# One image of the sixth pair stored over two queues, and four small rows in place of seven

## The chip, the cores and the metric

The kernel runs on one core of a Trainium2 chip. The metric is device time of one execution in microseconds (us), the median of several executions. Lower is better.

## The reference

A dilated 3x3 convolution, written as loops:

```python
batch, c_in, h, w, c_out, k, dilation = 16, 64, 64, 64, 128, 3, 2
x_pad = np.pad(x, ((0, 0), (0, 0), (pad, pad), (pad, pad)))     # pad = 2
for b, co, ci, kh, kw in all combinations:
    output[b, co] += weight[co, ci, kh, kw] * x_pad[b, ci, kh*2:kh*2+h, kw*2:kw*2+w]
```

Input `x` is 16 images of 64 channels of 64x64 (float32, 16.8 MB), the output 16 images of 128 channels of 64x64 (float32, 33.6 MB).

## The kernel before

The 16 images are worked on as 8 pairs. A pair of inputs lies on 128 partitions (two images of 64 channels), 16 KB in each. `load(pb)` brings one pair by one DMA of 128 rows of 16 KB. ScalarE and, for some chunks, GpSimd cast it to float16 (`cast`); VectorE forms sums of row blocks (`rowsum`); for pairs 3 to 5 ScalarE and GpSimd also make shifted copies (`shift`).

Each pair is computed in 4 groups `g` of 16 rows, 32 groups `G` in all. In every group TensorE makes three products, `psP`, `psA` and `psB`. ScalarE copies `psP` to SBUF (L307). VectorE adds it to `psA` and to `psB` (L315) and writes the results into a ring `o_ring` that holds the outputs of 3 pairs: pair 7 reuses the place of pair 4, and nothing reuses the place of pair 5. The order of all this is written out by hand (`manual_schedule`).

All transfers, loads and stores, are issued by SyncE in program order. A store of one whole image (`store`, L251) has 128 rows of 16 KB, one for each output channel, which is one for each partition. `pair_store(pb)` stores the two images of a pair after the last group of the pair, image 0 and then image 1. The transfers use 8 completion semaphores in turn, so a transfer is issued only when the one issued eight places earlier on that queue has landed.

The last pair is stored in halves. Its image 1 is stored differently in the first half (32 of 64 rows of pixels): `ROWS4` pixel rows at the end of that half are cut off and stored by two DMAs of their own, one of 124 partitions and one of the last 4 (`FOUR`). With `ROWS4 = 7` the main part has rows of 6,400 bytes, and the two cut-off stores have rows of 1,792 bytes.

```python
store(pb, 1, 0, 2 * GR - ROWS4)
store(pb, 1, 2 * GR - ROWS4, 2 * GR, FOUR)
```

The last two stores, of 128 rows of 8 KB each, follow when the last group is done.

Of the kernel before, what the change touches and what calls it, by code (L numbers as in the profile page):

```python
# [10 lines left out]
def kernel(  # L11
# [7 lines left out]
    nc = tc.nc  # L19
# [9 lines left out]
    P = 128  # L29
# [5 lines left out]
    HW = H * W  # L35
    GR = 16
# [19 lines left out]
    out_img = out.rearrange("b o h w -> b o (h w)")  # L56
# [14 lines left out]
    def o_pair(pb):  # L71
        at = pb % OB * 2 * HW
        return o_ring[:, at : at + 2 * HW]
# [80 lines left out]
    def turn(k):  # L154
# [24 lines left out]
        out=x16_tiles[0][:, 8 * W : 18 * W], in_=x32_tiles[0][:, 8 * W : 18 * W]  # L179
# [41 lines left out]
    for m in range(2):  # L221
        for r in range(2):
# [3 lines left out]
                out=w_st[pp, m * KW * CO : (m + 1) * KW * CO],  # L226
                in_=w_sb[pp, kind * KW * CO : (kind + 1) * KW * CO],
# [21 lines left out]
    def store(pb, m, r0=0, r1=H, rows=((0, P),)):  # L249
        for lo, hi in rows:  # L250
            nc.sync.dma_start(  # L251
                out=out_img[2 * pb + m, lo:hi, r0 * W : r1 * W],
                in_=o_pair(pb)[lo:hi, m * HW + r0 * W : m * HW + r1 * W],
            )

    def pair_store(pb):
        for m in range(2):
            store(pb, m, GR // 4 if pb == m == 0 else 0)

    LOADS = {0: (3,), 2: (4,), 3: (5,), 7: (6,), 11: (7,)}  # L260
    FOUR = ((0, P - 4), (P - 4, P))
    ROWS4 = 7

    for G in range(ngroups):
        pb, g = divmod(G, NG)
# [48 lines left out]
        for e, ps in ((1, psB), (0, psA)) if late else ((0, psA), (1, psB)):  # L314
            nc.vector.tensor_tensor(  # L315
                out=o[:, :, b0 : b0 + NBLK, e],
# [6 lines left out]
        if g == NG - 1 and later:  # L323
            pair_store(pb)
# [4 lines left out]
        if pb == npairs - 1:  # L329
            if g % 2 == 1:  # L330
                store(pb, 0, (g - 1) * GR, (g + 1) * GR)
                if g == 1:
                    store(pb, 1, 0, 2 * GR - ROWS4)
                    store(pb, 1, 2 * GR - ROWS4, 2 * GR, FOUR)
                else:
                    store(pb, 1, (g - 1) * GR, (g + 1) * GR)
        elif g == NG - 1 and not later:
            pair_store(pb)
# [35 lines left out]
```

## Time and profile before

| what | value |
|---|---|
| median of 3 runs | 126.7 us (126.54 to 127.01) |
| the profiled execution | 126.72 us |
| its span, first to last instruction | 124.9 us |
| bytes read from HBM, written to HBM | 17.07 MB, 33.55 MB |
| PE, DVE, ACT, POOL busy | 107.7, 90.8, 69.6, 31.0 us |
| SyncE's queue of transfers, share of 16 engines' span | 96.5% |

The page of the profile gives busy time by engine, the span in 40 slices, the transfers by queue, the chain of work that ended last, and the costliest groups of instructions. Besides, the trace holds one record for each packet of the DMA engines (queue, start, duration, size; not the number of the engine) and the time of each increment that a transfer makes to its semaphore: one for each DMA engine that took part. In this trace a packet is one row of a transfer. The core has 16 DMA engines; a store of 128 rows gives 8 rows to each.

### The profile page before, as it was taken

How to read it: one execution, taken by the hardware profiler on the slowest of the kernel's cores; microseconds unless marked ns; L12 is line 12 of the kernel's file. 1: busy time of each engine (PE TensorE's matmuls, PEld its weight loads, DVE VectorE, ACT ScalarE, POOL GpSimd, SP SyncE). 2: the span in 40 equal slices, each digit the busy share in tenths (PEclk: the TensorE clock that was granted, in tenths of full speed). 3: DMA queues.
4: the chain of work that ended last, by engine and by line, in shares of the span. 5: the costliest groups of instructions: out<-in, count | busy, mean ns of one | idle time of the engine just before them, and what ended most of it. 6: DMA issues, size and time to landing. Idle time of an engine off the chain costs nothing.

```text
span 124.9 us, 2265 instructions
## 1 busy us (share of the span) xinstructions
PE 107.7 (86%) x928; PEld 53.5 (43%) x928; DVE 90.8 (73%) x103; ACT 69.6 (56%) x76; POOL 31.0 (25%) x54
## 2 busy tenths in 40 slices
PE   6889999989999999999999999999999999920000
PEld 2255555545555553444444444445555555500000
DVE  0575979759998888596969797887988988760000
ACT  4178687396666887696848496949643333300000
POOL 3483306059610003829191920000000000000000
PEclk9999999999999999999999999999999999999555
DMA  4999999999899999999999999999999999999981
GB/s 118 402 445 446 435 414 430 435 435 409 291 410 442 425 441 425 417 430 425 438 435 422 435 420 420 430 441 430 430 430 420 425 430 435 425 422 412 420 380 76
DMA packets 4322, 50.77 MB, mean 406 GB/s; under 512 B 472, under 2 KB 728, under 8 KB 1112
## 3 DMA queue, kind: packets, MB, share of 16 engines
q1 hardware_dynamic: 4312, 50.63, 96.5%
q8 instruction: 7, 0.11, 0.3%
q14 instruction: 3, 0.02, 0.0%
HBM read 17.07 MB, written 33.55 MB: 405 GB/s over the span
## 4 chain that ended last, share of the span: by engine, by line
PE 66%; DVE 1%; DVEq 1%; issue 0%
PE psB L211 25%; PE psP L211 14%; PE psA L211 14%; PE psA L237 13%; DVE osb L315 1%; DVEq L369 1%; DVEq L315 0%
## 5 line engine op out<-in xcount | busy, mean ns | idle before, releaser
L211 PEld LDWEIGHTS <-w_sb 64*128 64x128 f16 x816 | 44.7, 94 | 42.0 <-issue 4.5
L315 DVE TENSOR_TENSOR osb<-psA,p_sb 128x1024 f32<-128x1024 f32 x32 | 39.1, 1223 | 15.6 <-ACT p_sb L307 11.9
L307 ACT COPY p_sb<-psP 128x1024 f32<-128x1024 f32 x32 | 32.4, 1012 | 30.5 <-issue 16.1
L211 PE MATMUL psB<-x,w_sb 64*128 64x496 f16 (+3 forms) x384 | 45.0, 365 | 0.0
L315 DVE TENSOR_TENSOR osb<-psB,p_sb 128x1024 f32<-128x1024 f32 x32 | 39.0, 1219 | 0.4 <-ACT p_sb L307 0.3
L83 ACT CAST x<-x 128x1024 f16<-128x1024 f32 (+2 forms) x27 | 28.2, 1050 | 4.1 <-DMA x<-in_x_dram 3.9
L118 POOL COPY xo<-x 64x512 f16<-64x512 f16 (+1 forms) x36 | 22.0, 612 | 28.9 <-PE psA L237 22.0
L211 PE MATMUL psA<-x,w_sb 64*128 64x496 f16 (+2 forms) x240 | 28.2, 365 | 0.3 <-DVE x L178 0.3
L211 PE MATMUL psP<-xs,w_sb 64*128 64x496 f16 (+1 forms) x192 | 26.0, 372 | 0.6 <-ACT p_sb L307 0.5
L237 PE MATMUL psA<-xo,w_st 128*128 128x496 f16 (+1 forms) x72 | 16.3, 375 | 0.0
L95 DVE TENSOR_TENSOR xs<-x 128x512 f16<-128x512 f16 x32 | 14.4, 450 | 0.2 <-ACT x L83 0.2
L237 PEld LDWEIGHTS <-w_st 128*128 128x128 f16 x72 | 6.6, 98 | 9.3 <-issue 2.1
L116 ACT COPY xo<-x 64x512 f16<-64x512 f16 x12 | 7.4, 615 | 0.2
L85 POOL CAST x<-x 128x896 f16<-128x896 f32 (+1 forms) x4 | 3.9, 987 | 8.5 <-DMA x<-in_x_dram 8.5
L136 PE MATMUL dm<-zero 128*128 128x512 f16 x10 | 4.6, 580 | 1.2 <-DVE zero L126 1.2
L225 POOL COPY w_st<-w_sb 64x384 f16<-64x384 f16 x4 | 2.5, 632 | 1.6 <-ACT w_sb L171 1.4
L146 DVE CAST wd<-w 128x192 f16<-128x192 f32 x1 | 0.5, 501 | 2.6 <-DMA w<-in_weight_dram 2.6
L136 PEld LDWEIGHTS <-zero 128*128 128x128 f16 x10 | 1.1, 124 | 2.6 <-issue 1.3
L159 PEld LDWEIGHTS <-wd 128*64 128x64 f16 x30 | 1.1, 128 | 2.3 <-DVE wd L146 1.2
L159 PE MATMUL wt<-ident,wd 128*64 128x128 f16 x30 | 1.7, 252 | 0.3 <-DVE wd L146 0.3
L148 ACT ACT_TABLE_LOAD x1 | 1.3, 1283 | 0.7 <-PEq L355 0.7
L171 ACT CAST w_sb<-wt 128x384 f16<-128x384 f32 x1 | 0.5, 479 | 1.9 <-PE wt L159 1.9
(19 smaller groups left out, 8.0 us busy)
## 6 DMA issues: line engine op xcount, KB each, us to landing
out_dram<-osb SPq DMA_DIRECT2D x13, 2048.0 KB, 18.6
x<-in_x_dram SPq DMA_DIRECT2D x7, 2048.0 KB, 14.7
out_dram<-osb SPq DMA_DIRECT2D x3, 1024.0 KB, 12.1
out_dram<-osb SPq DMA_DIRECT2D x1, 1920.0 KB, 18.9
x<-in_x_dram SPq DMA_DIRECT2D x1, 1088.0 KB, 5.3
x<-in_x_dram SPq DMA_DIRECT2D x1, 960.0 KB, 7.1
out_dram<-osb SPq DMA_DIRECT2D x1, 800.0 KB, 13.6
w<-in_weight_dram SPq DMA_DIRECT2D x1, 288.0 KB, 2.9
```

The costliest lines, as they stand in the source:

```text
L83: eng.copy(out=out, in_=in_)
L85: eng.tensor_copy(out=out, in_=in_)
L95: nc.vector.tensor_tensor(out=s, in0=v[:, :, 0], in1=v[:, :, 1], op=add)
L116: eng.copy(out=to, in_=src)
L118: eng.tensor_copy(out=to, in_=src)
L136: nc.tensor.matmul(out=dm[:, 0:512], lhsT=zero[:, 0:P], rhs=zero)
L159: nc.tensor.matmul(out=wts[k % 3][r * CI : (r + 1) * CI, c0 + j * CO : c0 + (j + 1) * CO], lhsT=wd[:, t * CI : (t + 1) * CI], rhs=ident,)
L211: nc.tensor.matmul(out=po, lhsT=w_sb[pp, t * CO : (t + 1) * CO], rhs=rhs, start=first and j == 1, stop=last and j == 2,)
L225: nc.gpsimd.tensor_copy(out=w_st[pp, m * KW * CO : (m + 1) * KW * CO], in_=w_sb[pp, kind * KW * CO : (kind + 1) * KW * CO],)
L237: nc.tensor.matmul(out=rows(ps[:, m * NH : (m + 1) * NH])[:, :, o0:o1], lhsT=w_st[:, t * CO : (t + 1) * CO], rhs=rows(xo[:, g, m])[:, :, d ...
L307: nc.scalar.copy(out=p_sb, in_=psP)
L315: nc.vector.tensor_tensor(out=o[:, :, b0 : b0 + NBLK, e], in0=ps.rearrange("p (m b q) -> p m b q", m=2, q=2 * W), in1=pv, op=add,)
```

## The change

Image 1 of pair 5 (`SHARED`; pairs are counted from 0) is no longer stored by one DMA of 128 rows on SyncE's queue. GpSimd issues two DMAs for it, of 5 rows and of 44 rows; SyncE issues five, of 64, 4, 4, 4 and 3 rows. Every row is 16 KB as before, and every row is stored once. With the rows counted in eights, the first DMA of GpSimd takes one row from each of the first five eights, its second takes the four odd rows from each of the other eleven. SyncE's DMA of 64 takes the even rows, its three DMAs of 4 take the other three odd rows of each of the first four eights, and its DMA of 3 takes those of the fifth eight.

In the last pair `ROWS4` becomes 4: the main part of that half image has rows of 7,168 bytes instead of 6,400, and the cut-off stores have rows of 1,024 bytes instead of 1,792.

No instruction of TensorE, VectorE or ScalarE changes, nor its place. GpSimd's two DMAs stand behind its last `shift` copy; SyncE has four more DMAs, between the store of image 0 of pair 5 and those of pair 6.

```diff
+    SHARED = (5, 1)
+
+    def shared_store(pb, m):
+        dst, src = out_img[2 * pb + m], o_pair(pb)[:, m * HW : (m + 1) * HW]
+        nc.gpsimd.dma_start(out=dst[1:40:8], in_=src[1:40:8])
+        nc.gpsimd.dma_start(out=dst[41:P:2], in_=src[41:P:2])
+        nc.sync.dma_start(out=dst[0:P:2], in_=src[0:P:2])
+        for k in (3, 5, 7):
+            nc.sync.dma_start(out=dst[k:32:8], in_=src[k:32:8])
+        nc.sync.dma_start(out=dst[35:40:2], in_=src[35:40:2])
+
     def pair_store(pb):
         for m in range(2):
-            store(pb, m, GR // 4 if pb == m == 0 else 0)
+            if (pb, m) == SHARED:
+                shared_store(pb, m)
+            else:
+                store(pb, m, GR // 4 if pb == m == 0 else 0)
...
-    ROWS4 = 7
+    ROWS4 = 4
```

## The prediction

> **What bounds the kernel now.** I read the page first: the busy lines, the slices, the queues. TensorE is busy for 86% of the span, but look at the last slices.
>
> ```profile
> PE   6889999989999999999999999999999999920000
> ...
> DMA  4999999999899999999999999999999999999981
> ...
> q1 hardware_dynamic: 4312, 50.63, 96.5%
> q8 instruction: 7, 0.11, 0.3%
> q14 instruction: 3, 0.02, 0.0%
> ```
>
> TensorE stops four slices early; the DMA engines are full from the second slice to the last but one. So the transfers set the end. The stretches of time say how full:
>
> ```profile
> core 0: us, PE busy (x) PEld busy (x) DVE busy (x) ACT busy (x) POOL busy (x), PEclk, DMA share, GB/s
> ...
> 113.00:118.00 5.00, 0.00 (x0) 0.00 (x0) 0.00 (x0) 0.00 (x0) 0.00 (x0) 0.72 1.01 420
> 118.00:121.00 3.00, 0.00 (x0) 0.00 (x0) 0.00 (x0) 0.00 (x0) 0.00 (x0) 0.50 0.98 412
> 121.00:124.90 3.90, 0.00 (x0) 0.00 (x0) 0.00 (x0) 0.00 (x0) 0.00 (x0) 0.50 0.30 126
> ```
>
> The share is 1.0 until 118, and 0.30 in the last 3.9 us: the 16 engines do not end together. The waits of SyncE's queue end in the same thing; its other long waits are for results of VectorE, with a backlog of transfers in front:
>
> ```profile
> SPq L251 <- DVE xs L95: 66.5, 7, 12.9
> SPq L369 <- DMA out_dram<-osb: 10.9, 3, 6.2
> ```
>
> The chain that ended last names 66% PE. It is followed back from VectorE's last add, done at 111.4, and does not contain the landing that the end waits for, so I don't use it.
>
> **Who ends last.** The increments of the last store (one for each DMA engine) come at 120.66, 120.93, 121.24, 121.25, 121.97, 122.02, 122.42, 122.54, 122.56, 123.06, 123.28, 123.53, 123.54, 123.54, 123.82 and 124.05. The span ends 0.90 later, the time stands 1.77 over the span. To know whose these are I chained packet records: an engine's next packet starts within about 5 ns of the end of the one before, and each has eight rows of every full store. That is a reconstruction; the records carry no engine number. It gives:
> - Four engines, and only four, carry the cut-off stores (31 rows and 1 row of 1,792 bytes each; both stores made four increments). They end at 123.06, 123.53, 123.54 and 123.82.
> - Of the twelve others one is slow in its own right: from 74 to 110 its 16 KB rows take 643 ns on average, on undisturbed engines 611. It ends last, 124.05.
> - The other eleven: 123.54, 123.28, then 122.56 and earlier. Those with a late end have had an instruction fetch (the q8 line) in their way.
>
> **The change, part by part.** The engines always have work queued, so what counts is the work given to each, by the medians of the row sizes: 16 KB 611 ns, 7,680 bytes 291, 6,400 bytes 244, 1,792 bytes 74, 1,024 bytes 46.
> - Main part of the half image: 7,168 bytes come to 272 ns between 244 and 291. Eight rows x 28 ns = +0.22 us on every engine.
> - Cut-off stores: 32 rows x (46 - 74) ns = -0.90 on the first four engines.
> - The moved rows, if they fall as the diff arranges them: +0.61 on engines 0 to 2, -1.83 on engine 4 (counted by the eights of rows), none elsewhere.
> - More completion records of 9 ns each: about +0.02, on the first four +0.03.
> - GpSimd's rows: four on engines 5 to 15, one on 0 to 4, on a second queue. No row of the trace shows a store on it. Lower bound 0 extra per row: a row moves the same bytes at the 611 ns that all undisturbed rows take, so a gain is excluded beyond the few ns between packets. Upper bounds are from the only other foreign packets, the fetches: an 8 KB fetch on q14 held its engine's own packets up for 302 ns and stretched the next by 115 to 349, that is 0.11 to 0.34 more than the 0.309 of an own row of that size; a 16 KB fetch on q8 held them up for about 0.9 and stretched the next by about 0.4, 0.66 more than 0.611. I take 0.11, the smallest seen: fetches read HBM singly, these rows read SBUF as stores do and queue behind each other. Call it x; four rows make 0.44, one 0.11.
>
> Sums, x apart: engines 0 to 2 -0.03, engine 3 -0.65, engine 4 -1.59, the others +0.24.
>
> The trace doesn't say which of the twelve is the slow one; by count alone it is engine 4 in one case of twelve. So the likeliest is that it keeps its eight rows: 124.05 + 0.24 + 0.44 = 124.73, 0.68 later, 126.72 + 0.68 = **127.4**. The profiled execution stands at the median (126.7), so nothing is corrected.
>
> **A rule on the slow engine.** The row is the 643 ns above. The Trainium skill, "DMA: Bandwidth & Descriptors", section "Latency and other measured facts", says engines 7 and 15 are usually the slower ones, which speaks against this change: by it engine 4 isn't the slow one, and the sum is the 127.4 above. The trace agrees that one engine is slow and that it isn't among the first four; it can't name it.
>
> **What costs nothing, and its cover.** GpSimd is idle after 72.7, and its DMAs wait for the add of the last group of pair 5, at 87.5; nobody waits behind them. SyncE's four more issues take 0.33 to 1.12 us each, at most 5 us from 87.5, and its next wish is at 99.1. A transfer waits for the one eight places earlier on its queue, and five small ones now stand among them. Pair 6's second store waits for pair 4's second, landed at 94.81; GpSimd's rows jump the backlog and make that 2.9 later, 97.7, wanted at 99.1. The half image at 105.7 waits for the 64-row part, by 105.4. With 8 us of backlog behind, a miss of 1 us would still cost nothing. VectorE writes pair 7 over pair 4 at 99.55: 1.8 us to spare.
>
> **Rivals.**
> 1. *The slow engine doesn't count: faster.* It is the spared one (then it ends near 122.5), or it isn't slow: its rows take 611 ns again from 54 to 58, from 69 to 74 and from 110 on, so the slowness comes and goes. Then the next count: engines 0 to 2 at 123.82 - 0.03 + x, and the others at 123.54 + 0.24 + 4x. At x = 0 the end is 123.79, -0.26: 126.46, and no version of this sum gives more. At x = 0.11 it is 124.22, +0.17: 126.9. The point that decides is x = 0.07. For it: the slow engine did end last, and a place that is slow in every execution could be spared on purpose. Against: five engines stand within 0.52 of it.
> 2. *GpSimd's rows fall on other engines: slower.* The two cut-off stores, with 124 and 4 rows, used the same four engines, so SyncE's queue begins at the first each time. If GpSimd's does the same with 44 rows on eleven engines, engines 0 to 2 have 13 rows instead of 8: 123.82 - 0.64 + 3.06 + 5x = 126.2 to 126.8, the time 128.9 to 129.5. If it deals three rows to each of engines 0 to 13 and two to the next, they have 12: 123.82 - 0.64 + 2.44 + 4x = 125.6 to 126.1, the time 128.3 to 128.7. The Trainium skill, same page, "Why a DMA increments its semaphore by 16 and not by 1", gives for GpSimd's queue eleven engines going on from a cursor, which is the diff's layout, and as a measured exception rows divided by 16 and rounded up, the three to each. No run here shows which.
> 3. *A foreign row is as dear as a fetch*, x = 0.66 on engines 5 to 15: 124.05 + 0.24 + 2.64 = 126.9, the time 129.6; at 0.34 it is 128.3.
> 4. *My chaining is wrong on who is last*, and the spared engine leads by over 0.6: near 125.9.
>
> **How the numbers follow.** Half a per cent, 0.63 us, is about what a measurement of this kernel can tell from no change: the limits are 126.07 and 127.33. The forecast has 0.34; at x under 0.1 it gives 126.96 to 127.3, within the limits, which is nearly half of it. Rival 1 has 0.26, nearly all within. Rival 2 0.20, rival 3 0.12, both slower. Rival 4 0.08, faster. That makes 0.08 faster, 0.38 within (0.15 + 0.23), 0.54 slower (0.19 + 0.03 + 0.20 + 0.12). The range takes in rival 1 from 126.4 and rival 2 to 128.8, and leaves out rival 4 and the dearest of 2 and 3.
>
> **What would show it.** After the change a second data queue with 49 packets of 16 KB. Right: 7,168-byte packets at 272 ns; the last increments again spread over about 3 us, the last from an engine with rows of 643 ns; one engine some 1.9 us earlier against the rest. Rival 1: the slow engine is that one. Rival 2: three engines end 1.7 us or more after all others. Rival 3: 16 KB packets well over 611 from 88 to 100 us, or holes between them. The forecast is wrong if the time is under 126.9, or if the DMA share falls under 1.0 between 100 and 118, which would mean a wait among the issues.

## The result and the profile after

The changed kernel takes 130.82 us against 126.75 before: the ratio is 1.0305, with an interval of 1.0267 to 1.0343. That is 4.1 us slower; the forecast was 127.4, and the range ended at 128.8. The profiled execution took 130.14, its span is 128.4 (before 126.72 and 124.9), so it shows 3.4 us of the loss. Executions fall into a faster and a slower state, so every ratio in this document compares the faster ones alone, while times are medians of all; e1 below has one fast execution and so no ratio, the ratio of e6 rests on two, and the profiles of these two runs, taken in the slower state, are not read.

The page after the change, the same lines as before (slices of 3.21 us; then queue, packets, MB, share of 16 engines' span):

```profile
PE   6889999989999999999999999999999999300000
...
DMA  4999999999899999999999999999999999999830
...
q1 hardware_dynamic: 4278, 49.83, 93.2%
q0 software_dynamic: 96, 0.80, 1.6%
q8 instruction: 7, 0.11, 0.3%
q14 instruction: 3, 0.02, 0.0%
```

TensorE is busy for 107.3 us (107.7 before). There is a second data queue, q0, with 0.80 MB, which is 49 rows of 16 KB. The loss is at the end, where the engines now run out one after the other. The stretches of time after the change (columns as in the prediction; the last two are DMA share and GB/s):

```profile
113.00:118.00 5.00, 0.00 (x0) 0.00 (x0) 0.00 (x0) 0.00 (x0) 0.00 (x0) 0.51 1.00 423
118.00:121.00 3.00, 0.00 (x0) 0.00 (x0) 0.00 (x0) 0.00 (x0) 0.00 (x0) 0.50 0.98 332
121.00:124.90 3.90, 0.00 (x0) 0.00 (x0) 0.00 (x0) 0.00 (x0) 0.00 (x0) 0.50 0.48 201
124.90:128.40 3.50, 0.00 (x0) 0.00 (x0) 0.00 (x0) 0.00 (x0) 0.00 (x0) 0.50 0.06 26
```

Two things are to be seen. Until 124.9 the engines have moved less than before, and from there on almost nobody works: a share of 0.06 is one engine of sixteen on average. And from 118 to 121 the engines count as full (0.98) but move 332 GB/s instead of 412: their packets take longer. Between 118 and 121, 28 of them (mostly 8 KB ones, up to 753 ns against 309) took over 100 ns more than is usual for their size; before, none did.

The issues came when the prediction said (start, us, engine, line). First GpSimd's queue of instructions, then SyncE's:

```profile
88.01 0.67 POOL L261 DMA_DIRECT2D out_dram<-osb  x1 [15.05 <-DVE osb L330]
88.68 0.53 POOL L262 DMA_DIRECT2D out_dram<-osb  x1
```

```profile
88.12 0.58 SPq L263 DMA_DIRECT2D out_dram<-osb  x1
88.75 3.08 SPq L265 DMA_DIRECT2D out_dram<-osb  x3
91.87 0.87 SPq L266 DMA_DIRECT2D out_dram<-osb  x1
99.29 14.03 SPq L251 DMA_DIRECT2D out_dram<-osb  x8
```

SyncE's waits after the change (total, times, longest):

```profile
SPq L384 <- DMA out_dram<-osb: 13.8, 1, 13.8
...
SPq L251 <- DMA out_dram<-osb: 1.0, 1, 1.0
```

One issue waited 1.0 us for a semaphore, the miss that the prediction allowed for; the DMA share stays at 0.98 or above until 118, so it cost nothing. The 13.8 is the wait for the last landing.

**Who ends last.** The last store's increments come at 120.87, 121.34, 121.44, 121.91, 122.26, 122.40, 122.74, 122.83, 122.95, 123.77, 124.32, 124.40, and then 125.16, 125.84, 126.65 and 127.15. Chained as in the prediction, the packets say that the last four are the four engines with the cut-off stores. They also say how GpSimd's rows fell: four to each of five engines, three to each of nine, two to one and none to one. That is one row to each of the first five, and of the 44 three to each engine from the first on, until they were used up. So engines 0 to 2 store 12 rows of this image, engine 3 has 11, engine 4 eight, the next nine 7, then one 6 and one 4. Of the five with four rows four are those of the cut-off stores; the fifth is the slow engine, whose 16 KB rows average about 647 ns here. If the DMAs of 4 and of 5 rows use the engines in order from the first, as this overlap suggests, it is engine 4, the one that was to be spared, and it stores eight rows as before. The records carry no engine number, so the 4 is a count and not a reading.

### The profile page after: what moved, and what is told of

Read it like the earlier page. It is cut to its first block, busy times and chain, and to the rows that moved or that the text cites. A ratio compares the mean times of both kernels' runs of the same rounds, so it can differ in the third digit from the quotient of the medians.

```text
span 128.4 us, 2272 instructions
## 1 busy us (share of the span) xinstructions
PE 107.3 (84%) x928; PEld 53.3 (42%) x928; DVE 90.8 (71%) x103; ACT 69.6 (54%) x76; POOL 32.1 (25%) x56
## 4 chain that ended last, share of the span: by engine, by line
PE 64%; DVE 1%; DVEq 1%; issue 0%
PE psB L211 24%; PE psP L211 14%; PE psA L211 13%; PE psA L237 12%; DVE osb L330 1%; DVEq L384 1%; DVEq L330 0%
## 5 line engine op out<-in xcount | busy, mean ns | idle before, releaser
L136 PE MATMUL dm<-zero 128*128 128x512 f16 x10 | 4.1, 533 | 1.2 <-DVE zero L126 1.2
L261 POOL DMA_DIRECT2D out_dram<-osb x1 | 0.7, 673 | 15.0 <-DVE osb L330 15.0
```

Of the source, the lines that this page charges most:

```text
L136: nc.tensor.matmul(out=dm[:, 0:512], lhsT=zero[:, 0:P], rhs=zero)
```

## The experiments

| run | time, us | ratio | interval |
|---|---|---|---|
| the change | 130.82 | 1.0305 | 1.0267 to 1.0343 |
| e1_two_small_pool | 131.89 to 135.43 | - | - |
| e2_even_queues | 126.91 | 0.9997 | 0.9960 to 1.0034 |
| e3_same_load_sync | 129.72 | 1.0198 | 1.0105 to 1.0291 |
| e4_rows4_only | 126.90 | 1.0000 | 0.9966 to 1.0034 |
| e5_halves | 131.07 | 1.0284 | 1.0209 to 1.0358 |
| e6_halves_sbuf_only | 132.07 | 1.0274 | 1.0160 to 1.0389 |
| e7_halves_hbm_only | 126.69 | 0.9977 | 0.9928 to 1.0026 |
| e8_skew_at_home | 125.71 | 0.9904 | 0.9856 to 0.9952 |
| e9_as_meant | 131.77 | 1.0394 | 1.0367 to 1.0420 |
| e10_away_alone | 128.36 | 1.0115 | 1.0089 to 1.0142 |
| e11_more_skew_at_home | 126.47 | 0.9990 | 0.9959 to 1.0020 |
| e12_load_at_home | 128.25 | 1.0116 | 1.0086 to 1.0145 |

The kernel before took 126.64 to 127.05 beside them (medians). The edits below are shortened: `dst` is the image in HBM, `src` its place in SBUF. Runs e1, e2, e4 to e7 and e10 edit the kernel before, the others the changed kernel.

### The second queue by itself: e2_even_queues

```diff
-nc.sync.dma_start(out=dst, in_=src)
+nc.gpsimd.dma_start(out=dst[1:P:2], in_=src[1:P:2])
+nc.sync.dma_start(out=dst[0:P:2], in_=src[0:P:2])
```

> Edit to the kernel before: image 1 of pair 5 is stored by one DMA of 64 rows on GpSimd's queue and one of 64 rows on SyncE's, so that each DMA engine has 4 rows on each queue and 8 in all, as before. ROWS4 stays 7. Theory 1 (the loss of the change is the load of the first engines, the second queue costs nothing by itself): 126.7, within 0.3. Theory 2 (what the loss has beyond the extra rows, some 1.5 us, is the price of rows on a second queue): 127.5 to 128.5, with 16 KB packets over 611 ns or holes between packets while both queues have rows.

No change. Its page has 64 rows on the second queue, and its stretch from 92 to 100 us, when both queues have rows, runs at the full rate (the first line is the kernel before, the second e2):

```profile
q0 software_dynamic: 80, 1.05, 2.0%
```

```profile
92.00:100.00 8.00, 8.00 (x82) 4.51 (x80) 7.01 (x9) 3.04 (x3) 0.00 (x0) 1.00 1.00 424
```

```profile
92.00:100.00 8.00, 8.00 (x81) 4.36 (x78) 7.17 (x8) 2.52 (x4) 0.00 (x0) 1.00 1.00 426
```

Of the 64 rows on the second queue 59 took 611 or 612 ns and one over 650 (985, close behind an instruction fetch). So a foreign row costs nothing measurable; theory 2 falls.

### The cut-off rows by themselves: e4_rows4_only

```diff
-    ROWS4 = 7
+    ROWS4 = 4
```

> Edit to the kernel before: ROWS4 = 4 alone. By the sums of the prediction engines 0 to 3 end 0.67 earlier, all others 0.22 later; the slow engine sets the end: 124.27, the time 126.9. If instead the smaller rows of 1,024 bytes bring the stretched packets that the changed kernel shows from 118 to 121, some 1 us: 127.7.

126.90, and the profiled execution's last increment at 124.40, where 124.27 was expected. By the chained packets the slow engine ends last. That agrees with the sum, but 0.2 us is less than the time can tell from nothing (1.0000, 0.9966 to 1.0034). What the run rules out is the other expectation, 127.7: the smaller rows by themselves do not bring the stretched packets, of which the profile has two.

### The same load without GpSimd: e3_same_load_sync

```diff
-nc.gpsimd.dma_start(out=dst[1:40:8], in_=src[1:40:8])
-nc.gpsimd.dma_start(out=dst[41:P:2], in_=src[41:P:2])
+nc.sync.dma_start(out=dst[39:P:2], in_=src[39:P:2])
+nc.sync.dma_start(out=dst[1:32:8], in_=src[1:32:8])
...
-nc.sync.dma_start(out=dst[35:40:2], in_=src[35:40:2])
+nc.sync.dma_start(out=dst[33:38:2], in_=src[33:38:2])
```

> Edit to the changed kernel: GpSimd stores nothing; all rows of image 1 of pair 5 are issued by SyncE, in DMAs of 64, 45, 4, 4, 4, 4 and 3 rows, which give the engines nearly the loads seen after the change: 12 rows to engines 0 to 2, 11 to engine 3, 7 to 4 to 14, 4 to engine 15. ROWS4 is 4. Theory 1 (load of the first engines alone): as slow as the changed kernel, 130 to 130.8. Theory 2 (part of the loss is the second queue): only the extra rows remain, +1.8 on the last of the first four engines, 128.4.

129.72: about two thirds of the loss comes back with no row on GpSimd's queue (2.0%, interval 1.05 to 2.9%). But it lies between the numbers of the two theories, and its 16 KB rows are stretched too, up to 1,754 ns between 100 and 106 us. What stretches them is the question of the runs below.

### Where GpSimd's rows begin: e1_two_small_pool and e9_as_meant

```diff
-nc.sync.dma_start(out=dst, in_=src)
+nc.gpsimd.dma_start(out=dst[0:5], in_=src[0:5])
+nc.gpsimd.dma_start(out=dst[5:16], in_=src[5:16])
+nc.sync.dma_start(out=dst[16:P], in_=src[16:P])
```

> Edit to the kernel before: image 1 of pair 5 is stored by two DMAs of GpSimd, of 5 and of 11 rows, and one of SyncE of 112 rows (7 to each DMA engine). ROWS4 stays 7. Theory A, GpSimd's queue deals the rows of every DMA from the first engine: engines 0 to 4 carry 2 rows on the second queue, engines 5 to 10 one, 11 to 15 none; engines 0 to 3 have 9 rows in all, +0.61, so the last increment moves from 124.05 to about 124.5 to 124.7 and the time to 127.2 to 127.4. Theory B, small counts go on from where the DMA before ended: every engine has exactly one row on the second queue, nothing is moved, the time is 126.7 plus at most 0.1.

131.9 and more: far off both theories. It couldn't tell them apart, since its 112 rows brought in something that neither had: from 16 on, seven to an engine, they are no longer each engine's own eight. Runs e5 to e7 are about that; the question itself was put again:

```diff
-nc.gpsimd.dma_start(out=dst[1:40:8], in_=src[1:40:8])
-nc.gpsimd.dma_start(out=dst[41:P:2], in_=src[41:P:2])
+Q = HW // 4
+for k in range(4):
+    nc.gpsimd.dma_start(out=dst[1:40:8, k*Q:(k+1)*Q], in_=src[1:40:8, k*Q:(k+1)*Q])
+    nc.gpsimd.dma_start(out=dst[41+2*k:P:8], in_=src[41+2*k:P:8])
```

> Edit to the changed kernel: GpSimd's 44 rows are issued as four DMAs of 11 rows (one row of each of the eights 5 to 15), and its 5 rows in four quarters of 4 KB, one ahead of each. Theory B (a small DMA on GpSimd's queue goes on from the engine where the last one ended): engines 5 to 15 store their own rows, the slow engine 4 has 5 rows, and the load is what the change says. By the sums engines 0 to 2 end at 123.8: 126.5, faster than before by 0.2. Theory A (every DMA begins at the first engine): engines 0 to 2 have 13 rows, 126.2 and so 128.9, and with rows away from their engine 130 and more.

131.77, on theory A's side. In the chained packets the five engines with 4 KB pieces (the four of the cut-off stores and the slow one) also have four of GpSimd's 16 KB rows each: a DMA of 11 rows after one of 5 begins at the first engine again. So in none of these forms can GpSimd's queue pass over engine 4.

### Rows away from their engine: e5_halves, e6_halves_sbuf_only, e7_halves_hbm_only

```diff
+# e5: rows 0 to 63, then 64 to 127, on both sides
+nc.sync.dma_start(out=dst[0:CI], in_=src[0:CI])
+nc.sync.dma_start(out=dst[CI:P], in_=src[CI:P])
+# e6: only the partitions that are read
+nc.sync.dma_start(out=dst[0:P:2], in_=src[0:CI])
+nc.sync.dma_start(out=dst[1:P:2], in_=src[CI:P])
+# e7: only the rows that are written
+nc.sync.dma_start(out=dst[0:CI], in_=src[0:P:2])
+nc.sync.dma_start(out=dst[CI:P], in_=src[1:P:2])
```

> Edit to the kernel before: image 1 of pair 5 is stored by two DMAs of SyncE, rows 0 to 63 and rows 64 to 127. Every DMA engine has 4 + 4 rows, 8 in all as before, but not the eight rows that it has in a store of 128 rows. ROWS4 stays 7. Theory 1 (load alone): 126.7, within 0.3. Theory 3 (an engine that works on rows of another engine's eight shares a path with it, and rows stretch from 611 to 1,000 ns and more, as some of the changed kernel's do): up to 8 rows x 0.5 us on top, 128 to 131, with stretched 16 KB packets from about 102 us on.

> As the halves, but only on the side of SBUF: the sources are partitions 0 to 63 and 64 to 127, the destinations the even and the odd rows, so that each engine writes rows of its own eight in HBM (the image's channels come out in another order). Theory 1: 126.7. Theory 3 with the shared path on SBUF's side: as slow as the halves. Theory 3 with the path on HBM's side: 126.7.

> The reverse: the sources are the even and the odd partitions, each engine reading its own eight, the destinations rows 0 to 63 and 64 to 127 (the image's channels come out in another order). Theory 1: 126.7. Theory 3 with the shared path on SBUF's side: 126.7. Theory 3 with the path on HBM's side: as slow as the halves.

All three give each engine eight rows. Two are 2.7 to 2.8% slower (the one with the halves in SBUF alone by 1.6 to 3.9%), the third is not slower at all. The stretch from 100 to 106 us, before, with halves on both sides, and with halves in HBM alone:

```profile
100.00:106.00 6.00, 6.00 (x60) 3.21 (x58) 5.17 (x7) 2.02 (x2) 0.00 (x0) 1.00 1.02 431
```

```profile
100.00:106.00 6.00, 6.00 (x60) 3.25 (x58) 5.17 (x7) 2.02 (x2) 0.00 (x0) 1.00 0.98 281
```

```profile
100.00:106.00 6.00, 6.00 (x60) 3.23 (x58) 5.17 (x7) 2.02 (x2) 0.00 (x0) 1.00 1.01 426
```

All are full by their share; one moves 281 GB/s. In it 46 rows took over 711 ns, the longest 2,589. So what counts is the partitions that are read, not the rows of HBM that are written. Even and odd rows, four of each consecutive eight at a time, are at full rate (e2, e7). The reading taken here is that a row is slow when an engine reads partitions outside its own consecutive eight ("away"), because another engine reads there too. That is argued and not shown: the records don't say which engine reads which partition, and no path was measured. A rival is that a contiguous half is slow because it reads only 64 of the 128 partitions at a time. By itself it is not enough, since the 112 rows of e1 span fourteen of the sixteen eights and that run lost 5 us or more; no run here separates the two further, and the next section has rows that fit neither.

### How much of it is in the change: e10_away_alone and e12_load_at_home

```diff
+# e10: 8 rows to each engine, four of them away
+nc.gpsimd.dma_start(out=dst[33:P:2], in_=src[33:P:2])
+nc.sync.dma_start(out=dst[0:P:2], in_=src[0:P:2])
+nc.sync.dma_start(out=dst[1:32:2], in_=src[1:32:2])
+# e12: 11 rows to engines 0 to 3, 7 to the others, all read at home
+nc.sync.dma_start(out=dst[0:P:2], in_=src[0:P:2])
+nc.sync.dma_start(out=dst[1:P:4], in_=src[1:P:4])
+nc.sync.dma_start(out=dst[3:P:8], in_=src[3:P:8])
+nc.sync.dma_start(out=dst[7:32:8], in_=src[7:32:8])
+for k in range(3):
+    nc.sync.dma_start(out=dst[39+32*k:min(P,71+32*k):8], in_=src[(1,3,5)[k]:32:8])
```

> Edit to the kernel before: image 1 of pair 5 is stored by one DMA of 48 rows on GpSimd's queue (odd rows 33 to 127, three to each engine) and two of SyncE, of 64 even rows and of 16 odd rows (1 to 31, one to each). Every engine has 8 rows, but four of them of another engine's eight, as the changed kernel's three or four are. ROWS4 stays 7. Load alone: 126.7. If rows away from their engine make what the extra rows of the changed kernel leave unexplained (about 1.5 us): 127.5 to 128.5, with stretched 16 KB packets from 93 to 105 us.

> Edit to the changed kernel: image 1 of pair 5 is stored by SyncE alone, and every engine reads only partitions of its own eight: DMAs of 64, 32 and 16 rows (4, 2 and 1 to each engine) and four DMAs of 4 rows by the first four engines, three of them with destinations in other eights (12 channels of the image get another channel's data). Engines 0 to 3 have 11 rows, the others 7: the load of the first engines after the change less one row, and no row read away from home. ROWS4 is 4. By load alone the first four end at 123.82 - 0.64 + 1.83 = 125.0: 127.7. The changed kernel is then this plus one row (0.6) plus what rows away from home cost (1.5 when alone). If load alone makes the whole loss, 129.5 and more.

Rows away alone cost 1.15%, 1.5 us; load alone, with one row less than in the change, 1.16%, also 1.5 us, half a microsecond over its sum. With the missing row (0.6 us, 0.5%) they make 2.8% of the 3.05% measured; the rest is within the intervals. The split is rough: it adds costs that were measured apart, and by the count in eights e10 has 57 rows away, the change 47.

From 100 to 106 us, with rows away (e10) and with the load read at home (e12):

```profile
100.00:106.00 6.00, 6.00 (x60) 3.19 (x56) 5.25 (x6) 2.02 (x2) 0.00 (x0) 1.00 1.02 399
```

```profile
100.00:106.00 6.00, 6.00 (x61) 3.23 (x58) 5.17 (x7) 2.02 (x2) 0.00 (x0) 1.00 1.01 415
```

Nor is e12 load alone. Four of its 16 KB rows took 716 to 2,101 ns between 101 and 103 us, and six rows of e11 below took 841 to 1,232, though by the count in eights every row of both is read at home; before, no 16 KB row in that stretch took over 711 ns except the one behind an instruction fetch. So either an engine's own partitions are not these eights, or rows are stretched by something else as well, which stays open.

### The skew by itself: e8_skew_at_home and e11_more_skew_at_home

```diff
+# e8: 7 rows to engines 0 to 3, 4 to the others
+nc.sync.dma_start(out=dst[0:P:2], in_=src[0:P:2])
+for k in (3, 5, 7):
+    nc.sync.dma_start(out=dst[k:32:8], in_=src[k:32:8])
+# e11: 8 rows to engines 0 to 3, 2 to the others
+nc.sync.dma_start(out=dst[0:P:4], in_=src[0:P:4])
+for k in (1, 2, 3, 5, 6, 7):
+    nc.sync.dma_start(out=dst[k:32:8], in_=src[k:32:8])
```

> Edit to the changed kernel: GpSimd's two DMAs and the one of 3 rows are left out, so 52 of the 128 rows of this image are not stored. Engines 0 to 3 have 7 rows, the twelve others 4, all of their own eights: the first four stand 3 rows behind the others, as after the change, without a row away from its engine. ROWS4 is 4. By load the first four end at 123.82 - 0.64 - 0.61 = 122.6 and the slow engine at 124.05 + 0.24 - 2.44 = 121.9: 125.3. Theory 4 (the skew between engines by itself brings the stretched packets of 118 to 121): about 1 us more, 126.3, with 8 KB packets over 309 ns.

> Edit to the changed kernel: image 1 of pair 5 is stored by SyncE alone, two rows of every eight by one DMA of 32 rows, and the six others of the first four eights by six DMAs of 4 rows; the other 72 rows are not stored. Engines 0 to 3 have 8 rows, the others 2, every row at home, a skew of six. ROWS4 is 4. By load the first four end at 123.82 - 0.64 = 123.2: 126.1. If the cut-off stores, when the first four are this far behind, stretch packets of their own engines as they do from 118 to 121 after the change: 127.

125.71 and 126.47, each 0.4 above its sum by load and under the 126.3 and 127 of the rival. In both, 8 KB and smaller packets are stretched behind 113 us as from 118 to 121 after the change (15 and 27 of them by over 100 ns), and the runs scatter (125.25 to 126.94, 125.93 to 127.57), up to 1.6 over the sum. What the stretched packets cost is not settled: the profiled execution of e8 has its 15 and took 125.25, no more than the sum. Nor is the skew shown to cause them, since e2, with eight rows to each engine, has 13 (up to 1,311 ns), and the kernel before has none. The cut-off stores, whose 31 rows to an engine are read across four or five eights, are the obvious suspects; that was not tested apart.

## Why the prediction was wrong

**Right.** The transfers set the end and TensorE does not. The row times of the cut-off stores and the main part held: 7,168 bytes took 272 ns and 1,024 bytes 46 (medians after the change), and e4, which was to end at 124.27 with the slow engine last, ended at 124.40, though its time can't tell that shift from none. GpSimd's and SyncE's issues were hidden as said. The sign was right, though not for the reason given: the forecast's 0.68 us was the main part's 0.24 and x, and neither made the loss.

**Wrong, the step that failed: "the moved rows, if they fall as the diff arranges them".** They didn't. The forecast took the diff's layout; GpSimd's 44 rows were dealt by threes from the first engine, rival 2 in its second form, which had a part of 0.20. So -0.03 on engines 0 to 2 was +1.80 by rows. The four engines with the cut-off stores ended last, at 125.16 to 127.15, all others by 124.40, and e12, with that load but one row, is 1.5 us slower by itself. The Trainium skill, "DMA: Bandwidth & Descriptors", "Why a DMA increments its semaphore by 16 and not by 1", has both the cursor and the dealing by rounded-up sixteenths, as an exception; the packets agree with the exception, and e9 shows no cursor for 5 and 11 rows either. The row that pointed there, the two cut-off stores beginning at the same four engines, was in the prediction and was given too little.

**Wrong, a term that was missing.** Rival 2's 128.3 to 128.7 is still 2 us short. All sums priced a row at 611 ns whichever engine reads it. When the rows of one store are dealt to other engines, they are not worth 611 each: the store costs 1.5 us more in e10 and about 3.6 in e5. The trace of before could not show it, because all its 16 KB rows belong to transfers of 128 rows, dealt alike. Why such rows are slower stays open, as said above.

**Wrong, x.** The price of a row on a second queue was taken as 0.11 from the instruction fetches. e2 shows none: its rows on that queue took 611 ns, and four of them to each engine gave 0.9997 (0.9960 to 1.0034, whose upper end is 0.43 us or 0.11 a row). The stretched packets that were to show rival 3 did appear after the change (720 to 1,124 ns between 93 and 97 us, on both queues, and again from 103 to 106), but not in e2, and with no second queue in e3; so the queue isn't what stretches them.

**The slow engine.** The forecast let it be any of twelve. It is engine 4, counted as in the result: of the twelve it alone carries four of GpSimd's rows after the change, and a slow engine has the 4 KB pieces in e9. The sentence of the Trainium skill on engines 7 and 15 ("DMA: Bandwidth & Descriptors", "Latency and other measured facts") is not borne out here. So the change aimed at the right engine, which the forecast had held unlikely, and it kept its eight rows for another reason; that the forecast left it at eight rows was right by luck. That such a spare would have gained at most 0.26 us (rival 1) could not be tested: no tried form of a DMA passes over engine 4.

## What to carry to other kernels

Before moving rows between DMA engines, find out which engine takes which row: count increments, and chain packets. A DMA cut to another row count or start is not the same transfer in smaller pieces, since each engine then reads other partitions; here even and odd rows cost nothing and contiguous halves 2.8%. A full DMA share is no full rate: read the GB/s beside it.

## What the hardware showed that was not expected

- Storing an image by two contiguous halves of the partitions (e5) stretched 16 KB rows from 611 ns to as much as 2,589 and took the core's rate from 431 to 281 GB/s; halves of the rows in HBM alone made no difference (e7, 426 GB/s).
- GpSimd's DMAs of 5, 11 and 44 rows all began at the engine at which SyncE's small DMAs begin; 44 rows went three to an engine.
- One DMA engine of sixteen was slow in stretches, 643 ns for a row of 611; in the two executions where its place could be told (the change and e9) it came right behind the four of the cut-off stores, engine 4 by count.
